# A two-layer streaming encoder: x turned by VectorE and carried through DRAM at five of six norms, blocks in another order, turned blocks issued from GpSimd

## The chip, the cores and the metric

One NeuronCore of a Trainium2 chip runs the kernel. Times are device microseconds (us). The engines are TensorE (PE: matmuls and transposes against an identity), VectorE (DVE), ScalarE (ACT), GpSimd (POOL) and SyncE (SP), which issues transfers. Each engine works its own instructions in a fixed order and waits on semaphores.

## The reference

x is (256, 1024) f32, two layers. Each layer does

```
x = x + 1/2 * SwiGLU_1(RMSNorm(x))      # D_FF = 2816
h = RMSNorm(x); [q_s|k_s|v_s|q_m] = h @ W_in
self attention (layer 0: chunked, relative bias; layer 1: differential, rotary)
memory attention: 4 heads into RMSNorm(mem) @ W_mem_kv
x = x + concat(self_out, mem_out) @ W_out
x = x + 1/2 * SwiGLU_2(RMSNorm(x))
```

with `swiglu(h) = (silu(h @ w_gate) * (h @ w_up)) @ w_down` and `rmsnorm(x, g) = x * rsqrt(mean(x^2) + eps) * g`. So six norms stand between products: three per layer.

## The kernel before

The 256 tokens are two blocks (tb 0, 1) of 128. Every dense product (`dense`) is three f32r matmuls of 128x512: each operand is split into a rounded part (h, hi) and a rest (l, lo), and hi·xh, lo·xh and hi·xl are summed in PSUM. Weights come in chunks of 1 MB (`raw`, three buffers; transfers from SyncE). A chunk has four quarters of 128x512; ACT rounds each into `hi` (L302), DVE makes `lo` (L314). There are four buffers for hi and lo, so at most four chunks are split ahead of use.

Norm and turn: a block is summed from PSUM in two halves of 512 columns (`finish`, L466 and L469). `prep_half` then turns a half by four TensorE transposes into the PSUM tile `xtp` (L396), multiplies by the gain (`y`, L427), rounds to `xh` on ACT (L430) and subtracts to `xl` on DVE (L432). The factor rsqrt(mean) is not applied to x but behind the next product: ACT squares (L441), DVE adds (`sst`, L450; `v`, L401), GpSimd takes the power (`xr`, L403).

A feed-forward runs eleven groups of 256 gate and 256 up columns (`gu`, two chunks each), eight k-steps for each block; in the first group all of block 0 goes before block 1 (but not in the first feed-forward). `evac` makes silu·up (`h`, L494), turns it by DVE in 32x32 blocks (`hb`, L503), stores it to DRAM (`hd`, L508) and loads it back with the blocks exchanged (`hr`, four loads, L514), both issued from SyncE; ACT and DVE split it to `ht`. The down product (`acc`) takes chunks 0 to 7 for all four (block, half) sums and the last three chunks (`SPLIT = NG - 3`) half by half, so that the sums of the four halves end one after the other and each norm half starts under the next. The mixer projects five column blocks (`proj`), each block 0 then block 1, runs the attention units beside them, and ends with the output product in the same manner.

The order of all instructions is written when the program is built: `Flow` keeps a clock with a cost for each operation, threads (`yield` of a time or a condition) are resumed when their condition holds on that clock, and `dense` steps it. At run time only each engine's order and the semaphores count.

Of the kernel before, what the change touches and what calls it, by code (L numbers as in the profile page):

```python
# [12 lines left out]
F32 = mybir.dt.float32  # L13
# [7 lines left out]
P = 128  # L21
# [6 lines left out]
KT = D // P  # L28
# [114 lines left out]
def kernel(  # L143
# [45 lines left out]
    load_x(0, 0)  # L189

# [61 lines left out]
    dma_free = [2.3]  # L252
# [10 lines left out]
    def loader():  # L263
        for i, c in enumerate(chunks):
# [4 lines left out]
            for j, (dst, src) in enumerate(c.parts):  # L269
                nc.sync.dma_start(out=dst(c.raw), in_=src)  # L270
                dma_free[0] += 2.9 / len(c.parts)
                if j == 1 and i < 2:
                    c.early = dma_free[0] + LAT
                    if i:
                        load_x(1, 1)
                        dma_free[0] += 0.7
            c.arrive = dma_free[0] + LAT
            if i == 0:
                load_x(1, 0)
                load_x(0, 1)  # L280
                dma_free[0] += 1.4
# [135 lines left out]
    def prep_half(xt, tb, hf, gc, wait=0.0):  # L417
        yield banks.has()
        tp = bank("xtp")
        for k in range(4):  # L420
            t = turn(tp[:, k, :], xs[tb][:, hf * 512 + k * P:hf * 512 + (k + 1) * P])
        yield t
        yield g2.has()
        y = g2.take([P, 4, P], F32, "y")
        ks = slice(hf * 4, hf * 4 + 4)
        g = gcol[:, gc + hf * 4:gc + hf * 4 + 4]
        nc.vector.tensor_tensor(out=y, in0=tp, in1=g.unsqueeze(2).broadcast_to([P, 4, P]), op=ALU.mult)  # L427
        banks.give()
# [31 lines left out]
    def finish(acc, tb, xt, gc, half):  # L460
        for hf in range(2):
            sl = slice(hf * 512, (hf + 1) * 512)
            yield lambda: acc.t[tb][hf] is not None
            yield acc.t[tb][hf]
            if half:
# [6 lines left out]
            if xt is None:  # L472
                nc.sync.dma_start(out=out[0, tb * P:(tb + 1) * P, sl], in_=xs[tb][:, sl])
            else:
                yield from prep_half(xt, tb, hf, gc)


    def ffn(l, nm, xt, gc_next):
# [3 lines left out]
        def evac(g, ps, end):  # L482
# [23 lines left out]
            hd = dram.tile([4, 32, 4, P], F32, tag="hd", name="hd")  # L506
            yield t
            nc.sync.dma_start(out=hd.rearrange("a i b x -> (a i) (b x)"), in_=hb.rearrange("p b f t j -> p (b f t j)"))  # L508
            yield flow.now + 3.0
            g2.give()  # L510
            yield g2.has()
            hr = g2.take([P, 4, 2, 2, 32], F32, "hr")
            for b in range(4):
                nc.sync.dma_start(out=hr[32 * b:32 * b + 32].rearrange("p a f t j -> p a (f t j)"),  # L514
                                  in_=hd[:, :, b, :].rearrange("a i x -> i a x"))
            yield flow.now + 4.0
            yield g4.has()
            ht = g4.take([P, 2, 4, P], F32R, "ht")
            src = hr.rearrange("p a f t j -> p (f t) a j")
# [8 lines left out]
        for g, ids in enumerate(plan[l, nm, "gu"]):  # L528
# [6 lines left out]
            for tb, c in order:  # L535
# [4 lines left out]
                if c == 1:  # L540
                    end[tb] = t
# [799 lines left out]
```

## Time and profile before

| | |
|---|---|
| median of 3 runs | 974.63 us (974.41 to 975.08) |
| profiled execution | 975.12 us, its span 973.3 us, granted clock 1.000 |
| PE, DVE, ACT, POOL busy | 99%, 69%, 56%, 6% |
| DMA | 200.90 MB, mean 206 GB/s; 65.5% of the 16 engines' span in the one queue of transfers |
| transfers of turned blocks | 44 stores of 256 KB, 176 loads of 64 KB, all from SP |
| transposes of x on PE | 96 |

A row of the timeline is: start us, us, engine line operation out<-in shape xcount, and in brackets the idle time before it with what ended it. A row of the groups by line has busy us and mean ns, then the idle time in front. A row of the windows gives for a stretch the busy time and the count of PE, PEld (weight load), DVE, ACT and POOL, the granted clock, the DMA share and GB/s.

### The profile page before, as it was taken

To read this page: it belongs to the slowest core of one execution; us is meant where nothing else is said; L and a number is where in the kernel's file an instruction comes from. 1 tells how busy PE (TensorE), PEld (TensorE's weight loads), DVE (VectorE), ACT (ScalarE), POOL (GpSimd) and SP (SyncE) were. 2 spreads that over 40 slices of the span, in tenths; PEclk is the share of its full clock that TensorE was granted. 3 is DMA by queue.
4 is the path that set the end of the run, shared out by engine and by line. 5 is a ranking of instruction groups with operands and counts; after the bars stand their busy time and mean duration, and the time that the engine had idled before them with its cause. 6 is when DMAs were issued, how large, how long until landed. Compare 5 with 4: busy or idle time off the path is not lost.

```text
span 973.3 us, 13393 instructions
## 1 busy us (share of the span) xinstructions
PE 964.6 (99%) x4576; PEld 791.3 (81%) x4576; DVE 675.7 (69%) x1485; ACT 542.4 (56%) x1159; POOL 60.1 (6%) x65
## 2 busy tenths in 40 slices
PE   9999999999999999999999999999999999999998
PEld 7888888887777888888888888888787788888886
DVE  6776675887777866666476676644989886676641
ACT  6554544766685655445445555443677764555540
POOL 0000000022210000000000000000344100000000
PEclk9999999999999999999999999999999999999999
DMA  9989766475525567887648887764641369788641
GB/s 289 306 242 270 257 225 206 162 260 173 174 87 173 163 209 223 242 263 242 235 124 252 250 252 237 253 207 136 207 140 50 125 199 284 235 251 254 226 130 44
DMA packets 164447, 200.90 MB, mean 206 GB/s; under 512 B 9433, under 2 KB 140058, under 8 KB 164378
## 3 DMA queue, kind: packets, MB, share of 16 engines
q1 hardware_dynamic: 164378, 200.04, 65.5%
q8 instruction: 36, 0.59, 0.3%
q14 instruction: 33, 0.27, 0.1%
HBM read 187.42 MB, written 12.58 MB: 205 GB/s over the span
## 4 chain that ended last, share of the span: by engine, by line
PE 91%; DVE 5%; ACT 1%; DMA 1%; issue 0%; SPq 0%; ACTq 0%
PE gu L383 16%; PE gu L386 16%; PE gu L389 16%; PE acc L386 9%; PE acc L389 9%; PE acc L383 9%; PE pj L389 3%; PE pj L383 3%; PE pj L386 3%; DVE lo L314 2%; PE xtp L396 1%; PE S L983 1%; PE AV L1064 1%; PE kv L389 1%; PE kv L386 1%; PE kv L383 1%
## 5 line engine op out<-in xcount | busy, mean ns | idle before, releaser
L314 DVE TENSOR_TENSOR lo<-raw,hi 128x512 fp32r<-128x512 f32 x656 | 416.5, 684 | 161.5 <-ACT hi L302 161.3
L302 ACT CAST hi<-raw 128x512 fp32r<-128x512 f32 x656 | 365.4, 618 | 241.3 <-PE gu L389 117.9
L389 PE MATMUL gu<-hi,xl 128*128 128x512 f32 x704 | 274.3, 390 | 0.0
L383 PE MATMUL gu<-hi,xh 128*128 128x512 f32 x704 | 274.1, 389 | 0.0
L386 PE MATMUL gu<-lo,xh 128*128 128x512 f32 x704 | 274.0, 389 | 0.0
L389 PEld LDWEIGHTS gu<-hi,xl 128*128 128x128 f32 x704 | 132.2, 188 | 27.5
L383 PEld LDWEIGHTS gu<-hi,xh 128*128 128x128 f32 x704 | 132.2, 188 | 27.3
L386 PEld LDWEIGHTS gu<-lo,xh 128*128 128x128 f32 x704 | 132.2, 188 | 27.2
L383 PE MATMUL acc<-hi,ht 128*128 128x512 f32 x352 | 137.7, 391 | 0.0
L386 PE MATMUL acc<-lo,ht 128*128 128x512 f32 x352 | 137.3, 390 | 0.2 <-DVE lo L314 0.2
L389 PE MATMUL acc<-hi,ht 128*128 128x512 f32 x352 | 137.4, 390 | 0.0
L386 PEld LDWEIGHTS acc<-lo,ht 128*128 128x128 f32 x352 | 66.1, 188 | 14.1 <-DVE lo L314 0.7
L389 PEld LDWEIGHTS acc<-hi,ht 128*128 128x128 f32 x352 | 66.1, 188 | 13.7
L383 PEld LDWEIGHTS acc<-hi,ht 128*128 128x128 f32 x352 | 66.1, 188 | 13.5
L523 DVE TENSOR_TENSOR ht<-hr,ht 128x512 fp32r<-128x512 f32 x44 | 30.3, 688 | 55.0 <-ACT ht L521 55.0
L521 ACT CAST ht<-hr 128x512 fp32r<-128x512 f32 x44 | 27.1, 617 | 69.5 <-DMA hr<-hd 69.5
L389 PE MATMUL pj<-hi,xl 128*128 128x512 f32 x160 | 64.6, 404 | 0.0
L386 PE MATMUL pj<-lo,xh 128*128 128x512 f32 x160 | 63.6, 398 | 0.0
L383 PE MATMUL pj<-hi,xh 128*128 128x512 f32 x160 | 63.6, 398 | 0.0
L491 ACT ACTIVATE sil<-gu,xr 128x256 f32<-128x256 f32 x88 | 41.4, 470 | 17.5 <-PE gu L389 17.5
L503 DVE STREAM_TRANSPOSE hb<-h 128x128 f32<-128x128 f32 x176 | 44.1, 289 | 1.2
L494 DVE SCALAR_TENSOR_TENSOR h<-gu,xr,sil 128x256 f32<-128x256 f32 x88 | 42.2, 480 | 1.6
(167 smaller groups left out, 806.5 us busy)
## 6 DMA issues: line engine op xcount, KB each, us to landing
raw<-in_ffn_w_down_dram SPq DMA_DIRECT2D x44, 1024.0 KB
raw<-in_ffn_w_gate_dram SPq DMA_DIRECT2D x86, 512.0 KB
raw<-in_ffn_w_up_dram SPq DMA_DIRECT2D x86, 512.0 KB
raw<-in_w_in_dram SPq DMA_DIRECT2D x32, 512.0 KB
hd<-hb SPq DMA_DIRECT2D x44, 256.0 KB
hr<-hd SPq DMA_DIRECT2D x176, 64.0 KB
raw<-in_w_out_dram SPq DMA_DIRECT2D x8, 1024.0 KB
raw<-in_w_mem_kv_dram SPq DMA_DIRECT2D x4, 1024.0 KB
```

What stands on the lines that cost most here:

```text
L302: nc.scalar.copy(out=c.hi[:, sl], in_=c.raw[:, sl])
L314: nc.vector.tensor_sub(c.lo[:, sl], c.raw[:, sl], c.hi.bitcast(F32)[:, sl])
L383: nc.tensor.matmul(out=ps, lhsT=xh, rhs=wh, start=start, stop=False)
L386: nc.tensor.matmul(out=ps, lhsT=xh, rhs=wl, start=False, stop=False)
L389: nc.tensor.matmul(out=ps, lhsT=xl, rhs=wh, start=False, stop=stop)
L396: nc.tensor.transpose(out=dst, in_=src, identity=flip if flipped else ident)
L491: nc.scalar.activation(sil, ps[tb][:, 0:256], AF.Silu, scale=xt.r[tb])
L494: nc.vector.scalar_tensor_tensor(out=h, in0=ps[tb][:, 256:512], scalar=xt.r[tb], in1=sil, op0=ALU.mult, op1=ALU.mult)
L503: nc.vector.transpose(out=hb[:, :, f, tb, :], in_=h[:, f * P:(f + 1) * P])
L521: nc.scalar.copy(out=hi, in_=src)
L523: nc.vector.tensor_sub(lo, src, hi.bitcast(F32))
L983: nc.tensor.matmul(out=ss[e][:, pr, :nk], lhsT=q[rows, pr, :], rhs=k[rows, pr, :], start=i == 0, stop=i == len(passes) - 1)
```

## The change

1. `through_dram` is a new function: one store and four loads, issued from GpSimd. `evac` uses it for all 44 groups. `prep_half(far=True)` turns x by four DVE transposes (`xb`), carries it through DRAM (`xr`), and multiplies by the gain from SBUF. That way is taken for both blocks at the norms behind a feed-forward (three: both mixer norms, and layer 1's first), and for block 1 alone at the two norms behind a mixer. In all GpSimd issues 300 transfers. The very first norm is as before.
2. The first two gate/up groups go block by block: block 0 of both groups, then block 1 of both (before: only the first group did). The first feed-forward keeps to k-steps with the blocks in turn. Layer 1's first two projections likewise.
3. `SPLIT = NG - 4`: the last four chunks of the down product go half by half (before: three).
4. At the start x's first half of block 1 is loaded ahead of the weights, with other start times of the four first halves; the warming matmuls are spread (not shown). At the end the output is added and stored in quarters of 256 columns, from SyncE and ACT in turn.

```diff
     load_x(0, 0)
+    load_x(1, 0)
...
-                    if i:
-                        load_x(1, 1)
-                        dma_free[0] += 0.7
             c.arrive = dma_free[0] + LAT
             if i == 0:
-                load_x(1, 0)
                 load_x(0, 1)
+                load_x(1, 1)
                 dma_free[0] += 1.4
             if i > 4 and late_done[0] < len(late_loads):
                 dst, src = late_loads[late_done[0]]
...
-    def prep_half(xt, tb, hf, gc, wait=0.0):
-        yield banks.has()
-        tp = bank("xtp")
-        for k in range(4):
-            t = turn(tp[:, k, :], xs[tb][:, hf * 512 + k * P:hf * 512 + (k + 1) * P])
-        yield t
+    def through_dram(src, name):
+
+        d = dram.tile([4, 32, 4, P], F32, tag="hd", name="hd")
+        nc.gpsimd.dma_start(out=d.rearrange("a i b x -> (a i) (b x)"), in_=src)
+        yield flow.now + 3.2
+        g2.give()
         yield g2.has()
-        y = g2.take([P, 4, P], F32, "y")
+        r = g2.take([P, 4, P], F32, name)
+        for b in range(4):
+            nc.gpsimd.dma_start(out=r[32 * b:32 * b + 32], in_=d[:, :, b, :].rearrange("a i x -> i a x"))
+        yield flow.now + 4.0
+        return r
+
+    def prep_half(xt, tb, hf, gc, wait=0.0, far=False):
         ks = slice(hf * 4, hf * 4 + 4)
         g = gcol[:, gc + hf * 4:gc + hf * 4 + 4]
-        nc.vector.tensor_tensor(out=y, in0=tp, in1=g.unsqueeze(2).broadcast_to([P, 4, P]), op=ALU.mult)
-        banks.give()
+        if far:
+            yield g2.has(2)
+            xb = g2.take([P, 4, 4, 32], F32, "xb")
+            for k in range(4):
+                nc.vector.transpose(out=xb[:, :, k, :], in_=xs[tb][:, hf * 512 + k * P:hf * 512 + (k + 1) * P])
+                t = flow.dve(128, 0.05)
+            yield t
+            xr = yield from through_dram(xb.rearrange("p b k j -> p (b k j)"), "xr")
+            yield g2.has()
+            y = g2.take([P, 4, P], F32, "y")
+            nc.vector.tensor_tensor(out=y.rearrange("p k (a j) -> p k a j", a=4),
+                                    in0=xr.rearrange("p a (k j) -> p k a j", k=4),
+                                    in1=g.unsqueeze(2).unsqueeze(3).broadcast_to([P, 4, 4, 32]), op=ALU.mult)
+            g2.give()
+        else:
+            yield banks.has()
+            tp = bank("xtp")
+            for k in range(4):
+                t = turn(tp[:, k, :], xs[tb][:, hf * 512 + k * P:hf * 512 + (k + 1) * P])
+            yield t
+            yield g2.has()
+            y = g2.take([P, 4, P], F32, "y")
+            nc.vector.tensor_tensor(out=y, in0=tp, in1=g.unsqueeze(2).broadcast_to([P, 4, P]), op=ALU.mult)
+            banks.give()
         yield flow.dve(512)
         nc.scalar.copy(out=xt.h[tb][:, ks, :], in_=y)
         yield flow.act(512)
...
-    def finish(acc, tb, xt, gc, half):
+    def finish(acc, tb, xt, gc, half, far):
         for hf in range(2):
             sl = slice(hf * 512, (hf + 1) * 512)
             yield lambda: acc.t[tb][hf] is not None
             yield acc.t[tb][hf]
+            if xt is None:
+                for q in range(2):
+                    qs = slice(hf * 512 + q * 256, hf * 512 + q * 256 + 256)
+                    nc.vector.scalar_tensor_tensor(out=xs[tb][:, qs], in0=acc.ps[tb][hf][:, q * 256:q * 256 + 256],
+                                                   scalar=0.5, in1=xs[tb][:, qs], op0=ALU.mult, op1=ALU.add)
+                    yield flow.dve(256)
+                    (nc.scalar if q else nc.sync).dma_start(out=out[0, tb * P:(tb + 1) * P, qs], in_=xs[tb][:, qs])
+                banks.give()
+                continue
             if half:
                 nc.vector.scalar_tensor_tensor(out=xs[tb][:, sl], in0=acc.ps[tb][hf], scalar=0.5, in1=xs[tb][:, sl],
                                                op0=ALU.mult, op1=ALU.add)
...
-            if xt is None:
-                nc.sync.dma_start(out=out[0, tb * P:(tb + 1) * P, sl], in_=xs[tb][:, sl])
+            if far and hf == 0:
+                flow.spawn(prep_half(xt, tb, hf, gc, far=True))
             else:
-                yield from prep_half(xt, tb, hf, gc)
+                yield from prep_half(xt, tb, hf, gc, far=far)
 
...
-            hd = dram.tile([4, 32, 4, P], F32, tag="hd", name="hd")
-            yield t
-            nc.sync.dma_start(out=hd.rearrange("a i b x -> (a i) (b x)"), in_=hb.rearrange("p b f t j -> p (b f t j)"))
-            yield flow.now + 3.0
-            g2.give()
-            yield g2.has()
-            hr = g2.take([P, 4, 2, 2, 32], F32, "hr")
-            for b in range(4):
-                nc.sync.dma_start(out=hr[32 * b:32 * b + 32].rearrange("p a f t j -> p a (f t j)"),
-                                  in_=hd[:, :, b, :].rearrange("a i x -> i a x"))
-            yield flow.now + 4.0
+            yield t
+            hr = yield from through_dram(hb.rearrange("p b f t j -> p (b f t j)"), "hr")
             yield g4.has()
             ht = g4.take([P, 2, 4, P], F32R, "ht")
-            src = hr.rearrange("p a f t j -> p (f t) a j")
+            src = hr.rearrange("p a (c j) -> p c a j", c=4)
...
-        for g, ids in enumerate(plan[l, nm, "gu"]):
+        def open_group(g):
             flow.until(banks.has(2))
-            ps = [bank(f"gu{tb}", (P, 512)) for tb in range(2)]
-            end = [None, None]
+            ps, end = [bank(f"gu{tb}", (P, 512)) for tb in range(2)], [None, None]
             flow.spawn(evac(g, ps, end))
-            order = [(tb, c) for tb in range(2) for c in range(2)] if g == 0 and (l, nm) != (0, 1) else \
-                    [(tb, c) for c in range(2) for tb in range(2)]
-            for tb, c in order:
-                for k in range(4):
-                    kk = 4 * c + k
-                    t = dense(ps[tb], xt.h[tb][:, kk, :], xt.l[tb][:, kk, :], lambda: xt.t[tb][kk], ids[c], k,
-                              lambda w: k4(w)[:, k, :], kk == 0, kk == KT - 1)
-                if c == 1:
-                    end[tb] = t
+            return g, ps, end
+
+        def run(grp, tb, kk):
+            g, ps, end = grp
+            c, k = kk // 4, kk % 4
+            t = dense(ps[tb], xt.h[tb][:, kk, :], xt.l[tb][:, kk, :], lambda: xt.t[tb][kk], plan[l, nm, "gu"][g][c], k,
+                      lambda w: k4(w)[:, k, :], kk == 0, kk == KT - 1)
+            if kk == KT - 1:
+                end[tb] = t
+
+        rest = 0
+        if (l, nm) == (0, 1):
+            grp = open_group(0)
+            for kk in range(KT):
+                for tb in range(2):
+                    run(grp, tb, kk)
+            rest = 1
+        else:
+            grps = []
+            for tb in range(2):
+                for g in range(2):
+                    if tb == 0:
+                        grps.append(open_group(g))
+                    for kk in range(KT):
+                        run(grps[g], tb, kk)
+            rest = 2
+        for g in range(rest, NG):
+            grp = open_group(g)
+            for c in range(2):
+                for tb in range(2):
+                    for k in range(4):
+                        run(grp, tb, 4 * c + k)
...
-        SPLIT = NG - 3
+        SPLIT = NG - 4
...
-            flow.spawn(finish(acc, tb, nxt, gc_next, True))
+            flow.spawn(finish(acc, tb, nxt, gc_next, True, True))
...
-        def proj(i, evac):
-            flow.until(banks.has(2))
-            ps = [bank(f"pj{tb}", (P, 512)) for tb in range(2)]
+        def proj(*parts):
+            pss = []
             for tb in range(2):
-                for c in range(2):
-                    for k in range(4):
-                        kk = 4 * c + k
+                for n, (i, evac) in enumerate(parts):
+                    if tb == 0:
+                        flow.until(banks.has(2))
+                        pss.append([bank(f"pj{j}", (P, 512)) for j in range(2)])
+                    ps = pss[n]
+                    for kk in range(KT):
+                        k = kk % 4
                         t = dense(ps[tb], xt.h[tb][:, kk, :], xt.l[tb][:, kk, :], lambda: xt.t[tb][kk],
-                                  plan[l, "in"][i][c], k, lambda w: k4(w)[:, k, :], kk == 0, kk == KT - 1)
-                flow.spawn(evac(ps[tb], tb, t))
+                                  plan[l, "in"][i][kk // 4], k, lambda w: k4(w)[:, k, :], kk == 0, kk == KT - 1)
+                    flow.spawn(evac(ps[tb], tb, t))
 
         class Heads:
             def __init__(self):
...
             flow.spawn(unit(c, tb))
-        proj(0, qk_evac(0))
-        flow.until(g4.has(2))
-        take_v()
-        proj(1, v_evac)
-        proj(2, qk_evac(1))
-        proj(3, qk_evac(2))
-        proj(4, vq_evac)
+        if typ_a:
+            proj((0, qk_evac(0)))
+            flow.until(g4.has(2))
+            take_v()
+            proj((1, v_evac))
+        else:
+            flow.until(g4.has(3))
+            take_v()
+            proj((0, qk_evac(0)), (1, v_evac))
+        proj((2, qk_evac(1)))
+        proj((3, qk_evac(2)))
+        proj((4, vq_evac))
...
-            flow.spawn(finish(acc, tb, nxt, gc_next, False))
+            flow.spawn(finish(acc, tb, nxt, gc_next, False, tb == 1))
...
-            flow.spawn(start(tb, hf, (3.75, 8.2, 7.4, 10.4)[2 * tb + hf]))
+            flow.spawn(start(tb, hf, (3.75, 9.2, 4.6, 9.9)[2 * tb + hf]))
```

What it does to the order, at two places. VectorE at layer 1's norm behind the second feed-forward of layer 0, from block 0's last `y` to the first `h` of the next product (raw, hi and lo 86 to 88 are weight chunks; acc11 the last sum; xl0, xl1 the rests of block 0 and 1). Before:

```order
L427 TENSOR_TENSOR y_4910<-xtp_4898,gcol_103 128x512
L314 TENSOR_TENSOR lo86_4905<-raw86_4746,hi86_4904 128x512 x3
L432 TENSOR_TENSOR xl1_4486<-y_4910,xh1_4484 128x512
L466 SCALAR_TENSOR_TENSOR x1_86<-acc11_4482,x1_86 128x512
L314 TENSOR_TENSOR lo86_4905<-raw86_4746,hi86_4904 128x512
L314 TENSOR_TENSOR lo87_4925<-raw87_4783,hi87_4924 128x512 x2
L427 TENSOR_TENSOR y_4962<-xtp_4949,gcol_103 128x512
L314 TENSOR_TENSOR lo87_4925<-raw87_4783,hi87_4924 128x512 x2
L314 TENSOR_TENSOR lo88_4960<-raw88_4820,hi88_4959 128x512 x2
L432 TENSOR_TENSOR xl1_4486<-y_4962,xh1_4484 128x512
L314 TENSOR_TENSOR lo88_4960<-raw88_4820,hi88_4959 128x512
L494 SCALAR_TENSOR_TENSOR h_5001<-gu0_4932,xr_4489,sil_4993 128x256
```

Now, behind the last sum's add and one quarter of lo86:

```order
L435 STREAM_TRANSPOSE xb_4996<-x1_86 128x4x32 x4
L458 TENSOR_TENSOR xl0_4531<-y_4970,xh0_4529 128x512
L312 TENSOR_TENSOR lo86_4956<-raw86_4792,hi86_4955 128x512 x3
L476 TENSOR_TENSOR sst_5023<-xss_4533 128x1
L399 TENSOR_SCALAR v_5025<-sst_5023 128x1
L441 TENSOR_TENSOR y_5033<-xr_4989,gcol_104 128x512
L312 TENSOR_TENSOR lo87_4982<-raw87_4829,hi87_4981 128x512 x4
L458 TENSOR_TENSOR xl1_4532<-y_5033,xh1_4530 128x512
L529 SCALAR_TENSOR_TENSOR h_5070<-gu0_4975,xr_4535,sil_5054 128x256
L312 TENSOR_TENSOR lo88_5021<-raw88_4966,hi88_5020 128x512
L538 STREAM_TRANSPOSE hb_5072<-h_5070 128x4x32 x2
L441 TENSOR_TENSOR y_5081<-xr_5047,gcol_104 128x512
```

The last half's `y` moved from ahead of lo87's third quarter to behind lo88's first, since its data come back through DRAM, and block 0's second `xl` now stands behind the last sum.

GpSimd's queue at the same norm holds nothing but one power per block before. Now:

```order
L418 DMA hd_4862<-xb_4851 128x512
L424 DMA xr_4880<-hd_4862 32x4x128 x4
L418 DMA hd_4899<-xb_4888 128x512
L424 DMA xr_4920<-hd_4899 32x4x128 x4
L418 DMA hd_4950<-xb_4929 128x512
L424 DMA xr_4989<-hd_4950 32x4x128 x4
L418 DMA hd_5009<-xb_4996 128x512
L401 TENSOR_TENSOR xr_4535<-v_5025,nhalf_94 128x1
L424 DMA xr_5047<-hd_5009 32x4x128 x4
L401 TENSOR_TENSOR xr_4536<-v_5103,nhalf_94 128x1
L418 DMA hd_5195<-hb_5072 128x512
L424 DMA hr_5234<-hd_5195 32x4x128 x4
```

Each half's store stands behind the loads of the half before it, and the first power of the norm between the last half's store and its loads.

More of the change, by code (lines that the diff above doesn't have):

```diff
@@ L251 @@
     hl_left = [NHL]
-    dma_free = [2.3]
+    dma_free = [4.0]
     LAT = 1.5
@@ L1259, in start_gain @@
         warm(2)
-        yield 5.0
-        warm(6)
+        for t in (5.0, 5.6, 6.2, 6.8, 7.4):
+            yield t
+            warm(2)
     def start(tb, hf, t):
```

## The prediction, made before the changed kernel ran

> **What bounds the kernel now.** I read the page first (busy time, chain of waits), then windows and TensorE's own row, then groups by line, and last the places where the edits fall.
>
> ```profile
> PE 964.6 (99%) x4576; PEld 791.3 (81%) x4576; DVE 675.7 (69%) x1485; ACT 542.4 (56%) x1159; POOL 60.1 (6%) x65
> PE 91%; DVE 5%; ACT 1%; DMA 1%; issue 0%; SPq 0%; ACTq 0%
> 440.00:480.00 40.00, 40.00 (x178) 33.11 (x178) 22.60 (x41) 18.48 (x36) 0.00 (x0) 1.00 0.75 244
> 500.00:510.00 10.00, 10.00 (x48) 8.25 (x47) 9.96 (x20) 8.33 (x18) 0.00 (x0) 1.00 0.50 151
> 690.00:780.00 90.00, 87.82 (x502) 69.29 (x502) 81.25 (x184) 64.69 (x182) 30.89 (x27) 1.00 0.40 130
> ```
>
> TensorE (PE) is 91% of the chain and never idle between 440 and 480: 178 matmuls in 40.00 us, of which one or two straddle an edge, so 0.227 each. Yet the row 500 to 510, a norm, shows VectorE (DVE) at 9.96 of 10: PE does not wait there, but DVE has nothing left to give. Only layer 1's mixer (690 to 780) shows idle PE time, 2.2 us. So an edit pays by what leaves PE's row, and costs what it puts on DVE at a norm.
>
> **What is removed: 7.04 us of PE.**
>
> ```profile
> 503.37 0.39 PE L389 MATMUL gu<-hi,xl 128*128 128x512 f32 x1
> 503.60 0.39 PE L383 MATMUL gu<-hi,xh 128*128 128x512 f32 x1
> 503.83 0.39 PE L386 MATMUL gu<-lo,xh 128*128 128x512 f32 x1
> 504.06 0.60 PE L396 MATMUL xtp<-ident,x 128*128 128x128 f32 x4
> 504.41 0.47 PE L389 MATMUL gu<-hi,xl 128*128 128x512 f32 x1
> 504.72 0.39 PE L383 MATMUL gu<-hi,xh 128*128 128x512 f32 x1
> L396 PE MATMUL xtp<-ident,x 128*128 128x128 f32 x96 | 15.0, 280 | 0.9 <-DMA x<-in_x_dram 0.9
> ```
>
> From the matmul before four turns (503.83) to the second after them (504.72) is 0.89 instead of two pitches, 0.45: a set of four costs 0.44. 96 turns are 24 sets; TensorE's order keeps 8, so 16 × 0.44 = 7.04 goes. Regrouped matmuls (the later split of the down projection, blocks, `proj`) keep their number: 0.
>
> **What is added on DVE.** Per half block four transposes of x, where y already existed.
>
> ```profile
> 502.68 0.69 DVE L466 SCALAR_TENSOR_TENSOR x<-acc,x 128x512 f32<-128x512 f32 x1
> 503.28 1.89 DVE L314 TENSOR_TENSOR lo<-raw,hi 128x512 fp32r<-128x512 f32 x3
> 505.08 0.69 DVE L427 TENSOR_TENSOR y<-xtp,gcol 128x512 f32<-128x512 f32 x1
> 505.69 2.49 DVE L314 TENSOR_TENSOR lo<-raw,hi 128x512 fp32r<-128x512 f32 x4
> 509.69 0.15 DVE L450 TENSOR_TENSOR sst<-xss 128x1 f32<-128x1 f32 x1
> 509.95 0.68 DVE L314 TENSOR_TENSOR lo<-raw,hi 128x512 fp32r<-128x512 f32 x1
> 510.55 0.50 DVE L503 STREAM_TRANSPOSE hb<-h 128x128 f32<-128x128 f32 x2
> ```
>
> Back to back a 128x512 operation starts every 0.60 (502.68, 503.28; three in 1.80), a transpose takes 0.25, so four take 1.0. Sixteen halves add 16 us of DVE, of no price in itself; what counts is when DVE's row, in its fixed order, delivers the lo quarters that PE wants next. I walk it at layer 1's first norm behind a feed-forward. Time 0 is the end of the last down matmul; the half before it ended 24 × 0.227 = 5.44 earlier (24 matmuls by the new split). DVE after that earlier end: add done −4.7, xl −4.1, transposes −3.1, four lo85 −0.7, y −0.1; then, with the last half: add 0.75, lo86's first 1.35, transposes 2.35, xl 2.95, three lo86 4.75, the two small ones 5.05, y 5.65, four lo87 8.05 (the first at 6.25), xl 8.65, h 9.05, lo88's first 9.65, two transposes 10.15, y 10.75, lo88's second 11.35.
>
> PE needs lo87's first quarter one matmul into the second group, 5.44 + 0.23 = 5.67: 0.58 late. Half a group on (2.72), lo88's first is due at 8.97, comes 9.65: 0.68. Its second is due three matmuls later, 10.33, comes 11.35: 1.02. Sum **+2.28**. Before, PE took two chunks in these 10.87 us, now four, because block 0 runs both groups; that is the price of the block order. At the mixer's norm of layer 1 the same walk, with the head sums (0.6) in place of h, gives 0.58 + 1.05 + 0.44 = **+2.07**. At layer 0's mixer norm the memory products (two stretches of 10.87) stand between: 0. At the two norms behind a mixer only block 1 goes through DRAM: layer 0 nothing, layer 1 the block-0 half's xl about 3.63 against 3.17 due, so **+0.5** (bounds 0 and 2). Transposes and y inside layer 1's mixer: 0 taken, since PE waits there anyway and DVE has 8.75 of 90 free; bounds 0 and 2.4 (four 0.6 operations).
>
> **What is moved: five transfers per group and per half to GpSimd.** The trace of before has no transfer from GpSimd, so its issue price e is bounded by what stands nearest.
>
> ```profile
> L514 SPq DMA_DIRECT2D hr<-hd x176: 312/427/1487, 30.8 to 916.5; - x176
> L403 POOL TENSOR_TENSOR mr<-v,nhalf 128x1 f32<-128x1 f32 x2 | 1.1, 550 | 163.1 <-DVE v L401 163.1
> L403 POOL TENSOR_TENSOR xr<-v,nhalf 128x1 f32<-128x1 f32 x12 | 8.8, 732 | 435.6 <-DVE v L401 435.6
> L403 POOL TENSOR_TENSOR of<-v,nhalf 128x2 f32<-128x2 f32 x6 | 5.9, 991 | 21.9 <-DVE v L401 21.9
> 510.18 0.86 POOL L403 TENSOR_TENSOR xr<-v,nhalf 128x1 f32<-128x1 f32 x1 [10.67 <-DVE v L401]
> 419.28 0.34 SPq L508 DMA_DIRECT2D hd<-hb  x1
> 421.32 1.75 SPq L514 DMA_DIRECT2D hr<-hd  x4
> 427.09 0.62 ACT L521 CAST ht<-hr 128x512 fp32r<-128x512 f32 x1 [4.08 <-DMA hr<-hd]
> 343.17 1.75 SPq L514 DMA_DIRECT2D hr<-hd  x4
> 346.64 0.62 ACT L521 CAST ht<-hr 128x512 fp32r<-128x512 f32 x1 [1.85 <-DMA hr<-hd]
> ```
>
> Low bound 0.43 (SyncE's issue), high 0.99 (a two-column GpSimd operation). I take 0.73, GpSimd's smallest operation in the very norms concerned. The store lands 421.32 − 419.28 − 0.34 = 1.70 after its issue; the loads 346.64 − 344.92 = 1.72 after their last issue, or 4.02 where weights stand ahead on SyncE's queue. On a queue of its own the first is nearer; with some share for the weights I take 2.2. A transport then takes 5e + 1.70 + 2.2 = 7.55, and holds GpSimd's queue 5e + 1.70 = 5.35, under the 5.44 between halves. The last half's store is issued at 2.45, lands at 10.0; DVE comes to its y at 10.15. It fits, barely: 0, as long as e stays under 0.75. GpSimd's own work queued behind (the two rsqrt per norm, the next group's five transfers) then moves by under one transport and the down projection uses those much later. The evacuation's transfers in the other groups are equally far from their use: 0, because the down projection starts only when all groups are through.
>
> By the Trainium skill (DMA: Bandwidth & Descriptors, "Queues, rings and completion order") each transfer engine turns between queues packet by packet, which would favour 1.72 over 4.02; no run here shows it yet. With 4.02 instead the sum would be 1.67 worse at each of four norms, as worked in the first rival.
>
> **Start and end.** x's first half of block 1 now stands ahead of the weights and warming matmuls are spread; 256 KB at the 289 GB/s of the page's first slice are 0.9, so 0 with bounds ±0.9. At the end the last add covers half the columns and is followed by its own store:
>
> ```profile
> 969.57 0.69 DVE L466 SCALAR_TENSOR_TENSOR x<-acc,x 128x512 f32<-128x512 f32 x1 [3.39 <-PE acc L389]
> 970.28 0.33 SPq L473 DMA_DIRECT2D out_dram<-x  x1
> GB/s 289 306 242 270 257 225 206 162 260 173 174 87 173 163 209 223 242 263 242 235 124 252 250 252 237 253 207 136 207 140 50 125 199 284 235 251 254 226 130 44
> ```
>
> Half of 0.69 can be won, another issue (0.33) lost: 0.
>
> **Sum.** −7.04 + 2.28 + 2.07 + 0.5 = −2.2. The profiled execution took 975.12 (span 973.3), so 972.9; the median of the three runs, 974.63, gives **972.4**.
>
> **Rivals.**
>
> *The transport comes late (slower).* Place: y of the last half in DVE's order, behind which lo88 waits, and behind that PE. For it: the row at 510.18, where the same rsqrt takes 0.86 rather than 0.55 beside a lo on DVE (509.95), and DVE is full at every norm. Against it: the mean there is 0.73. Past e = 0.75 a queue of four halves loses 5e + 1.70 − 5.44 at each of three intervals. At 0.86: 3 × 0.56 + (2.45 + 8.20 − 10.15) = 2.2 at each of two norms, 1.05 at each norm behind a mixer (one interval): +6.5 − 2.2 = +4.3, so 978.9. At 0.99: 4.8 and 2.35, +14.3 − 2.2, so **986.7**. It decides the sign from e = 0.79. Loads that land in 4.02 with e = 0.73 cost 1.67 four times: 979.1.
>
> By the Trainium skill (SBUF — State Buffer, "SBUF: two separate sides") a VectorE operation with two operands in SBUF shuts out a GpSimd instruction that reads SBUF, and certain VectorE operations starve transfers that GpSimd issues. The 0.86 agrees with the first half; no row here bears on the second. By it the result is this rival's 978.9 or more.
>
> *DVE loses nothing (full gain).* If operations ready early let lo run ahead of my walk, the stalls vanish: −7.04, so **967.6**. For: no PE wait at 500 to 510 although DVE is at 9.96. Against: twice the chunks in the same time. That the turns don't leave at all is ruled out by TensorE's order.
>
> **How the numbers follow.** Forecast 0.52, late transport 0.30, full gain 0.18. Within 0.2% (1.95 us, about what can be told from no change) the forecast lies just outside, so I split it 0.28 faster, 0.17 same, 0.07 slower; the late transport is 0.28 slower and 0.02 same. Faster 0.46, same 0.19, slower 0.35. The forecast's own range comes from its unknowns (start ±0.9, layer 1's entry −0.5 to +1.5, its mixer up to +2.4, seldom all at once): about 970.5 to 976. The range reaches from 966 (full gain and a good start) to 987 (e = 0.99).
>
> **What would show it.** Eight sets of turns in PE's groups; PE waits for lo of about 0.6, 0.7 and 1.0 in the second group behind the two norms of layer 1; GpSimd's issue in its queue's row (0.73; past 0.79 I am wrong in sign); y's release by DVE itself, not by a transfer; no PE wait at layer 0's mixer. Wrong I am if waits stand ahead of the down projection, or if DVE's transposes of x take longer than 0.25.

## The result: 8% slower

The changed kernel takes 1054.03 us in the median of 6 runs (1046.55 to 1057.57), the kernel before 974.77 in 6 runs beside it: a ratio of 1.0804, 95% interval 1.0769 to 1.0838. Forecast were 972.4 and a range up to 987. The profiled execution is the fastest of the six, with a span of 1044.8 us, so that its parts below add up to 71 us of loss and not to the 79 of the medians.

The page of the changed kernel, its busy times, its chain of waits, and three of its groups by line; the last row is the same group in the kernel before:

```profile
PE 984.9 (94%) x4520; PEld 791.3 (76%) x4520; DVE 682.6 (65%) x1553; ACT 534.2 (51%) x1159; POOL 225.0 (22%) x365
PE 32%; DMA 27%; ACT 12%; issue 11%; DVE 11%; POOL 6%; ACTq 0%; DVEq 0%; POOLq 0%
DMA hr<-hd 16%; ACT hi L300 9%; POOL hr L424 5%; DVE lo L312 5%; PE gu L381 4%; PE gu L387 4%; PE gu L384 4%; PE acc L384 3%; PE acc L387 3%; DMA hd<-hb 3%; PE acc L381 3%; DMA xr<-hd 2%; DMA hd<-xb 2%; PE pj L381 2%; PE pj L384 2%
...
L547 ACT CAST ht<-hr 128x512 fp32r<-128x512 f32 x44 | 27.3, 620 | 279.3 <-DMA hr<-hd 279.3
L441 DVE TENSOR_TENSOR y<-xr,gcol 128x512 f32<-128x512 f32 x16 | 11.0, 688 | 35.7 <-DMA xr<-hd 35.7
L394 PE MATMUL xtp<-ident,x 128*128 128x128 f32 x32 | 5.5, 309 | 0.0
```

```profile
L521 ACT CAST ht<-hr 128x512 fp32r<-128x512 f32 x44 | 27.1, 617 | 69.5 <-DMA hr<-hd 69.5
```

TensorE was 91% of the chain and is 32%. The longest other piece is not a norm: it is `hr<-hd`, the loads of the groups' turned blocks. ACT stood idle for 279.3 us ahead of the 44 casts that take them up, 6.3 each; before it was 69.5, 1.6 each. VectorE's wait for the halves of x is 35.7 over all 16. The turns did leave: 32 are left of 96.

Where the time went is read from TensorE's rows, part by part: from the first dense matmul of a part to the first of the next, in us of the profiled executions. The experiments below stand beside it.

| part | before | the change | e4: groups planned by landing | e1: all from SyncE | e7: e1 without the halves' way | e12: e1, 3 chunks held, weights held back | e16: one norm only |
|---|---|---|---|---|---|---|---|
| start | 9.0 | 8.9 | 8.3 | 8.4 | 8.6 | 8.4 | 8.7 |
| layer 0: gate/up 1 | 121.3 | 128.9 | 121.9 | 125.8 | 126.0 | 126.1 | 121.5 |
| down 1 | 63.7 | 79.2 | 68.0 | 67.6 | 69.1 | 62.2 | 63.7 |
| memory products | 23.0 | 28.9 | 28.8 | 29.7 | 25.6 | 33.1 | 23.0 |
| projections, attention | 71.4 | 71.4 | 71.4 | 71.4 | 71.4 | 71.6 | 71.4 |
| output product | 32.4 | 31.9 | 31.9 | 31.9 | 32.4 | 31.9 | 31.9 |
| gate/up 2 | 120.2 | 122.7 | 124.1 | 124.7 | 120.2 | 119.7 | 119.7 |
| down 2 | 61.3 | 66.6 | 59.8 | 59.8 | 61.3 | 60.1 | 61.3 |
| layer 1: gate/up 1 | 120.2 | 129.3 | 124.0 | 125.0 | 120.2 | 121.7 | 120.2 |
| down 1 | 61.3 | 66.1 | 59.8 | 59.8 | 61.3 | 60.6 | 61.3 |
| projections, attention | 73.3 | 77.9 | 78.5 | 75.9 | 68.0 | 69.4 | 73.3 |
| output product | 32.4 | 33.3 | 33.3 | 33.3 | 37.0 | 38.0 | 31.6 |
| gate/up 2 | 120.2 | 129.6 | 125.9 | 126.2 | 120.2 | 121.7 | 120.2 |
| down 2, to the end | 63.8 | 70.1 | 63.8 | 63.7 | 63.7 | 63.7 | 63.8 |

Every feed-forward is longer, its down product too, and that far from any norm. One group of layer 0 in the timeline of the changed kernel (POOL is GpSimd, SPq SyncE's queue):

```profile
104.01 0.56 POOL L418 DMA_DIRECT2D hd<-hb  x1 [10.23 <-DVE hb L538]
104.92 0.37 SPq L271 DMA_DIRECT2D raw<-in_ffn_w_gate_dram  x1
105.33 0.57 SPq L271 DMA_DIRECT2D raw<-in_ffn_w_up_dram  x1
106.70 2.17 POOL L424 DMA_DIRECT2D hr<-hd  x4 [2.13 <-DMA hd<-hb]
107.33 0.37 SPq L271 DMA_DIRECT2D raw<-in_ffn_w_gate_dram  x1
107.74 0.51 SPq L271 DMA_DIRECT2D raw<-in_ffn_w_up_dram  x1
116.47 0.62 ACT L547 CAST ht<-hr 128x512 fp32r<-128x512 f32 x1 [8.99 <-DMA hr<-hd]
117.00 3.22 ACT L300 CAST hi<-raw 128x512 fp32r<-128x512 f32 x6
118.72 0.56 POOL L418 DMA_DIRECT2D hd<-hb  x1 [9.85 <-DVE hb L538]
```

and the same group in the kernel before:

```profile
101.63 0.34 SPq L508 DMA_DIRECT2D hd<-hb  x1
103.78 1.80 SPq L514 DMA_DIRECT2D hr<-hd  x4
110.81 0.62 ACT L521 CAST ht<-hr 128x512 fp32r<-128x512 f32 x1 [0.56 <-DMA hr<-hd]
112.60 0.34 SPq L508 DMA_DIRECT2D hd<-hb  x1
```

From the store's issue to ACT's cast it was 9.18, with ACT waiting 0.56 of it. Now it is 12.46, and ACT waits 8.99. The issue price is a small part of it: the five issues took 2.14 and take 2.73. The loads are issued while two chunks of weights, 2 MB, are in flight or follow, and on another queue than those. In the trace's packet records the first packet of these loads comes 3.5 us after their issue, when the chunk ahead of them has gone, and then their 256 KB share the transfer engines with the next chunk for 5.3 us. Behind the cast, ACT has the weight casts (117.00, six at once) that TensorE and the raw buffers wait for. The next group's store follows 14.7 later, before 10.97 (101.63 to 112.60).

This closes a circle: a store, its late loads, ACT's cast, the weight casts and VectorE's work behind it, the next store. Over the 44 groups the cast came 8.9 us behind its store in the median before, and comes 11.4 behind it now; ACT was through with what stands ahead of the cast 8.3 us behind the store before, and 3.5 now. In the group shown TensorE loses nothing yet (14.00 of 14.00 us busy between 104 and 118), since it lives on chunks that were split ahead. It pays later, 0.69 behind the next cast, and more in the down product, behind the one after that:

```profile
146.60 0.62 ACT L547 CAST ht<-hr 128x512 fp32r<-128x512 f32 x1 [9.67 <-DMA hr<-hd]
147.13 3.22 ACT L300 CAST hi<-raw 128x512 fp32r<-128x512 f32 x6
147.79 0.50 PE L381 MATMUL acc<-hi,ht 128*128 128x512 f32 x1 [1.65 <-ACT hi L300]
```

Over the first feed-forward gate/up and down product together lose 23 us by the table. Not all of it is the groups': with their casts written later (e4 below) 4.9 of the 23 stay.

### The profile page after: what moved, and what is told of

It reads as the page before. It is cut to its first block, busy times and chain, and to the rows that moved or that the text cites. A ratio compares the mean times of both kernels' runs of the same rounds, so it can differ in the third digit from the quotient of the medians.

```text
span 1044.8 us, 13542 instructions
## 1 busy us (share of the span) xinstructions
PE 984.9 (94%) x4520; PEld 791.3 (76%) x4520; DVE 682.6 (65%) x1553; ACT 534.2 (51%) x1159; POOL 225.0 (22%) x365
## 4 chain that ended last, share of the span: by engine, by line
PE 32%; DMA 27%; ACT 12%; issue 11%; DVE 11%; POOL 6%; ACTq 0%; DVEq 0%; POOLq 0%
DMA hr<-hd 16%; ACT hi L300 9%; POOL hr L424 5%; DVE lo L312 5%; PE gu L381 4%; PE gu L387 4%; PE gu L384 4%; PE acc L384 3%; PE acc L387 3%; DMA hd<-hb 3%; PE acc L381 3%; DMA xr<-hd 2%; DMA hd<-xb 2%; PE pj L381 2%; PE pj L384 2%
## 5 line engine op out<-in xcount | busy, mean ns | idle before, releaser
L312 DVE TENSOR_TENSOR lo<-raw,hi 128x512 fp32r<-128x512 f32 x656 | 412.7, 681 | 32.4 <-ACT hi L300 32.2
L381 PE MATMUL gu<-hi,xh 128*128 128x512 f32 x704 | 277.0, 393 | 9.1 <-ACT xh L456 6.1
L547 ACT CAST ht<-hr 128x512 fp32r<-128x512 f32 x44 | 27.3, 620 | 279.3 <-DMA hr<-hd 279.3
L381 PE MATMUL acc<-hi,ht 128*128 128x512 f32 x352 | 140.5, 399 | 12.9 <-ACT hi L300 12.8
L384 PE MATMUL acc<-lo,ht 128*128 128x512 f32 x352 | 141.9, 403 | 9.2 <-DVE lo L312 8.3
L387 PE MATMUL acc<-hi,ht 128*128 128x512 f32 x352 | 139.1, 395 | 0.0
L424 POOL DMA_DIRECT2D hr<-hd x176 | 95.7, 550 | 127.2 <-ACT hi L300 56.5
L381 PEld LDWEIGHTS acc<-hi,ht 128*128 128x128 f32 x352 | 67.3, 191 | 31.5 <-ACT hi L300 17.6
L418 POOL DMA_DIRECT2D hd<-hb x44 | 25.0, 567 | 307.0 <-DVE hb L538 306.8
L387 PEld LDWEIGHTS acc<-hi,ht 128*128 128x128 f32 x352 | 67.4, 191 | 13.0
L456 ACT CAST xh<-y 128x512 fp32r<-128x512 f32 x24 | 14.7, 618 | 79.0 <-DVE y L441 68.4
```

The lines of the kernel that those rows point to most:

```text
L312: nc.vector.tensor_sub(c.lo[:, sl], c.raw[:, sl], c.hi.bitcast(F32)[:, sl])
L381: nc.tensor.matmul(out=ps, lhsT=xh, rhs=wh, start=start, stop=False)
L384: nc.tensor.matmul(out=ps, lhsT=xh, rhs=wl, start=False, stop=False)
L387: nc.tensor.matmul(out=ps, lhsT=xl, rhs=wh, start=False, stop=stop)
L418: nc.gpsimd.dma_start(out=d.rearrange("a i b x -> (a i) (b x)"), in_=src)
L424: nc.gpsimd.dma_start(out=r[32 * b:32 * b + 32], in_=d[:, :, b, :].rearrange("a i x -> i a x"))
```

## Experiments

Theory G: the groups' transfers cost, on a queue of their own beside the weights, through ACT's order. Theory N: the norms' new way costs.

**e1: all transfers from SyncE.**

```diff
 def through_dram(src, name):
-        nc.gpsimd.dma_start(out=d...., in_=src)
+        nc.sync.dma_start(out=d...., in_=src)
...
-            nc.gpsimd.dma_start(out=r[32 * b:32 * b + 32], ...)
+            nc.sync.dma_start(out=r[32 * b:32 * b + 32], ...)
```

> The change with all 300 transfers of turned blocks issued from SyncE instead of GpSimd, nothing else. Theory G (the groups' transfers are what costs: on a queue of their own they share the transfer engines with the weights, land late, and ACT's cast of ht holds the weight casts behind it): the 79 us go, 966 to 978. Theory N (the norms' new way through DRAM, with its extra VectorE work, is what costs): stays above 1030.

Measured: 1005.01, ratio 1.0298 (1.0281 to 1.0315). 49 us are gone, 30 stay: neither expectation held, each theory has a part.

**e2: groups from SyncE, norms from GpSimd.**

```diff
+        eng = nc.sync if name == "hr" else nc.gpsimd     # hr: a group's block
```

> The change with the 220 transfers of the 44 groups issued from SyncE, the 80 of the norms still from GpSimd. Theory G: 970 to 990. Theory N: above 1030.

Measured: 1001.71, ratio 1.0278 (1.0255 to 1.0301). That is above G's range and far under N's. The some 50 us belong to the groups; for the norms the queue makes hardly a difference.

**e3: the kernel before, groups from GpSimd.**

```diff
-            nc.sync.dma_start(out=hd....)
+            nc.gpsimd.dma_start(out=hd....)
...
-                nc.sync.dma_start(out=hr[32 * b:...])
+                nc.gpsimd.dma_start(out=hr[32 * b:...])
```

> The kernel before with only the 220 transfers of the 44 groups issued from GpSimd. Theory G: 1040 to 1065, alone as slow as the whole change. Theory N: 970 to 980.

Measured: 1041.82, ratio 1.0682 (1.0666 to 1.0698). Five transfers per group on another queue, and nothing else, cost 67 us, in G's range.

**e4: the change with one planner number altered.**

```diff
-        yield flow.now + 4.0
+        yield flow.now + (9.5 if name == "hr" else 4.0)
```

> The change with one planner number altered: the groups' loads are taken to need 9.5 instead of 4.0, so that ACT's cast of ht is written behind more weight casts; every transfer is still issued from GpSimd and lands as late. Theory G says that the late landing costs only through ACT's order: 970 to 1000. If the late landing costs by itself, or by less bandwidth for the weights: above 1030.

Measured: 1002.95, ratio 1.0284 (1.0268 to 1.03), 3 us past G's range and as good as moving the groups back. ACT's group in this kernel:

```profile
L547 ACT CAST ht<-hr 128x512 fp32r<-128x512 f32 x44 | 27.2, 617 | 0.0
```

ACT waits 0.0 us for the 44 loads though all still come from GpSimd, and three of the four down parts in the table are as in the kernel before or shorter (59.8, 59.8, 63.8); the first stays at 68.0, as with the groups on SyncE (67.6 in e1). The late landing cost only by the place where ACT's order took it up: that is what the groups cost. The rest, 28 us, is elsewhere.

**e10 and e11: the kernel before, only loads or only stores from GpSimd.**

```diff
-                nc.sync.dma_start(out=hr[32 * b:...])      # e10
+                nc.gpsimd.dma_start(out=hr[32 * b:...])
...
-            nc.sync.dma_start(out=hd....)                  # e11
+            nc.gpsimd.dma_start(out=hd....)
```

> The kernel before with the 176 loads hr issued from GpSimd, the 44 stores still from SyncE. Theory: the loads are the part that drains slowly beside the weights (5 us with about 1 MB of weights running, 2.2 us with none), so they carry nearly all of the 67 us: 1025 to 1045. Rival (GpSimd's issue and start of any transfer): half, about 1000 to 1015.

> The kernel before with the 44 stores hd issued from GpSimd, the loads still from SyncE. Theory: 974 to 985. Rival: about 1000 to 1015.

Measured: loads 1018.0, ratio 1.0421 (1.0375 to 1.0467); stores 975.54, ratio 1.0001 (0.999 to 1.0013). Stores from GpSimd are free, loads cost 43 of the 67, between the two ranges expected for them. Both together cost 24 more than the sum. The traces show a likely reason, not tested apart: in the median the cast comes 11.0 us behind the store's issue in e10 and 11.5 in e3, so once ACT waits for the loads, the store's part of the way counts too; with the loads on SyncE (e11) it is 8.6, and 8.9 before.

**The second part: e5 to e8.** Theory W: the four held down chunks and the block order stop the weights ahead of a norm. Theory F: the halves' way through DRAM is late by itself.

```diff
-        SPLIT = NG - 4          # e5: e1 with three chunks held
+        SPLIT = NG - 3
...
-            for tb in range(2):  # e6: e1, block order in the first group only,
-                for g in range(2):  # and one projection after the other
+            for tb in range(2):
...
-            flow.spawn(finish(acc, tb, nxt, gc_next, True, True))    # e7: e1, turns on TensorE
+            flow.spawn(finish(acc, tb, nxt, gc_next, True, False))
```

e8 is the kernel before with `through_dram` (from SyncE), `prep_half(far=True)` and the `far` of `finish` as the change has them, and nothing else of it.

> The all-SyncE version of the change with three instead of four down chunks kept for the half-by-half end, as before. Theory W (four held chunks fill all four hi and lo buffers, so no weight is split or fetched for 17 us ahead of a norm, and weights and turned halves then come together): gains most of the rest, 975 to 988. Theory F (the halves' way through DRAM is late by itself, since VectorE's y stands in its order ahead of lo): 1000 or more, because the halves now follow each other in 4.08 instead of 5.44.

> The all-SyncE version with only the first group block by block, as before, and the projections as before; four chunks still held. Theory W: a part of the rest, 985 to 998, since two chunks fewer are wanted in the first 10.87 us. Theory F: 995 to 1005.

> The all-SyncE version with all turns of x on TensorE again (the transposes come back: 7.0 us); blocks in the new order, four held chunks, new start and end stay. Theory F: the norms' loss goes, 975 to 985. Theory W: the loss stays, 995 to 1012.

> The kernel before with only the halves of the five norms turned by VectorE and carried through DRAM, all from SyncE; split, order of groups, start and end as before. Theory F: 985 to 1005. Theory W: 966 to 978.

Measured: e5 991.15, ratio 1.0161 (1.0141 to 1.0182); e6 1012.06, 1.0379 (1.0356 to 1.0402); e7 985.27, 1.0103 (1.0086 to 1.012); e8 1015.23, 1.0405 (1.0378 to 1.0431). All four miss the ranges: e5 lies between the two, e6 above both, e7 0.3 us and e8 10 us beyond F's. Still F holds for the larger part: without the halves' way (e7) the gate/up parts behind a norm are exactly as before, 120.2, block order and all; with nothing but it (e8) 40 us are lost. The block order does not cost: without it (e6) the halves' lateness costs 7 more. W has a part too, 14 us in e5. Where a half is late, all edits interact. Layer 1's first norm in e1, from the timelines of VectorE, SyncE and TensorE, and three windows:

```profile
516.26 0.34 SPq L418 DMA_DIRECT2D hd<-xb  x1
518.72 0.40 SPq L271 DMA_DIRECT2D raw<-in_ffn_w_gate_dram  x1
519.16 0.51 SPq L271 DMA_DIRECT2D raw<-in_ffn_w_up_dram  x1
519.71 3.04 SPq L424 DMA_DIRECT2D xr<-hd  x4
524.86 0.40 PE L381 MATMUL gu<-hi,xh 128*128 128x512 f32 x1
527.08 0.69 DVE L441 TENSOR_TENSOR y<-xr,gcol 128x512 f32<-128x512 f32 x1 [2.77 <-DMA xr<-hd]
527.69 2.49 DVE L312 TENSOR_TENSOR lo<-raw,hi 128x512 fp32r<-128x512 f32 x4
528.43 0.80 PE L384 MATMUL gu<-lo,xh 128*128 128x512 f32 x1 [3.17 <-DVE lo L312]
529.02 0.63 PE L387 MATMUL gu<-hi,xl 128*128 128x512 f32 x1
529.45 0.63 PE L381 MATMUL gu<-hi,xh 128*128 128x512 f32 x1
```

```profile
526.00:529.00 3.00, 0.57 (x1) 0.50 (x2) 1.92 (x4) 2.83 (x6) 0.00 (x0) 0.90 1.02 347
529.00:532.00 3.00, 3.00 (x9) 2.35 (x8) 3.00 (x7) 0.85 (x3) 0.00 (x0) 0.54 0.51 98
532.00:535.00 3.00, 3.00 (x14) 2.24 (x13) 2.96 (x6) 1.25 (x3) 0.00 (x0) 1.00 0.96 328
```

The half's store is issued at 516.26, its loads stand behind 1 MB of weights on SyncE and land at 527.08, 10.8 after the store. VectorE has stood there, and lo behind it, and TensorE behind lo. The same length shows in the change itself from GpSimd:

```profile
531.86 0.56 POOL L418 DMA_DIRECT2D hd<-xb  x1
536.73 0.56 POOL L418 DMA_DIRECT2D hd<-xb  x1
538.73 0.68 DVE L441 TENSOR_TENSOR y<-xr,gcol 128x512 f32<-128x512 f32 x1
547.57 0.69 DVE L441 TENSOR_TENSOR y<-xr,gcol 128x512 f32<-128x512 f32 x1 [3.52 <-DMA xr<-hd]
548.92 0.50 PE L384 MATMUL gu<-lo,xh 128*128 128x512 f32 x1 [3.95 <-DVE lo L312]
```

The second half, stored at 531.86 with no weights in flight, is taken up at 538.73, after 6.9; the third, stored at 536.73 with weights, at 547.57, after 10.8.

**e9: block order and quarters at the end alone.** Without any new transfer, three chunks held, start as before.

```diff
-    finish(..., far=True), SPLIT = NG - 4, new start
+    finish(..., far=False), SPLIT = NG - 3, start of before
```

> The change without its transfers: turns on TensorE, groups from SyncE, three held chunks, start as before; left of it are the block order of the first two groups and of layer 1's projections, and the end in quarters. If block order costs nothing (theory: the 2.28 and 2.07 that the prediction charged to it do not exist) 972 to 976. If they exist: 977 to 981.

Measured: 978.58, ratio 1.0034 (1.0021 to 1.0048), in the band that was to confirm the block order's price, and yet not by it: the gate/up parts behind norms are 120.2, 120.2 and 120.3 as before. Nearly the whole excess stands in the first gate/up (124.4 against 121.3), where TensorE waits 1.43 for x, having waited for it ahead of this part already, and 1.43 at the turn of the gain columns, one transpose of small loaded vectors. This turn stands behind 296 gate/up matmuls in TensorE's order, before and here alike; what moved is the last small load that it needs, which stands among the weights on SyncE and is issued at 72.3 before, at 75.6 here and at 77.3 in the changed kernel:

```profile
81.96 0.24 PE L231 MATMUL gps<-ident,grow 55*128 55x55 f32 x1 [4.62 <-DMA grow<-in_b_subln_dram]
```

In e3, with TensorE's order and the start of before, the load is issued at 80.7 and the wait is 7.70; in e4 there is none. So the groups' lateness alone can make it.

**e12: weights held back between a half's store and its loads.** e5 with

```diff
-            yield lambda: raw_left[0] > 0
+            yield lambda: raw_left[0] > 0 and hold[0] == 0     # hold: set from store to loads of a half
```

> The all-SyncE version with three held chunks, and in SyncE's order no weight transfer between a half's store and its loads at the five norms. Theory (a half turned through DRAM is late because its loads stand behind 1 MB of weights on SyncE's queue): 975 to 986, against 991 without the hold. If the loads are late by themselves, or the weights then are: 988 to 1000.

Measured: 990.12, ratio 1.0146 (1.0124 to 1.0167), in the rival's range. Yet the gate/up behind layer 0's mixer falls from 125.3 to 119.7, under the kernel before; the sum hides it behind other places: the gain columns, and the memory products at 33.1, where TensorE waits 7.9 for the normed memory keys (`kmn`), VectorE's work.

**e13 and e14: planner numbers by the measured landing.**

```diff
-        yield flow.now + 4.0                     # loads of a half, e13 on e12; e14 on e4 with three chunks held
+        yield flow.now + 7.5
...
-        yield flow.now + 8.0                     # gain columns
+        yield flow.now + 20.0
```

> As the version with weights held back (990), and two planner numbers nearer to the measured landing: a half's loads are taken to need 7.5 instead of 4.0, so that VectorE's y is written behind more of its other work, and the turn of the gain columns is written 12 us later. Theory (what is left of the loss is VectorE and TensorE standing at a transfer that the plan took to be there, above all 10 us at layer 0's mixer norm and 3 to 5 us at the gain columns): 974 to 982. Rival (TensorE itself needs the halves before they can land): 986 to 992.

> The change with all transfers from GpSimd as it stands, but planned by measured landings (groups' loads 9.5, halves' loads 7.5, gain columns 12 us later) and three held chunks. Theory (order, not the transfers, makes the loss): 976 to 990. Rival (shared transfer engines cost by themselves): 995 or more.

Measured: 1001.08, ratio 1.0262 (1.0242 to 1.0282), and 1016.55, ratio 1.043 (1.041 to 1.045): both worse than the kernels they start from, and e14 in its rival's range: the theory of order alone fell for the norms. Written later, the halves are taken later, and TensorE waits for xh itself (4.23 in one stretch ahead of layer 1's first gate/up in both), and for the memory keys 9.3 in e13 and 12.6 in e14. Only the gain columns were mended: the first gate/up is 121.1 and 121.4.

**e15: four held chunks, with all that was mended.** e12 with `SPLIT = NG - 4`, the gain columns' turn later, the memory's preparation at its old place.

> The all-SyncE change with its own split (four held chunks), no weight transfer between a half's store and its loads at the norms, the memory's preparation at its old place behind down chunk 6 and the gain columns' turn 12 us later. Theory (four held chunks give the halves their time, 5.44 apart, but stop the weights; three let the weights go on and leave the halves late): both costs stay apart from the mended ones, 984 to 992. If the hold alone was missing: 966 to 976.

Measured: 991.3, ratio 1.0157 (1.0142 to 1.0171), at the upper end of what was expected: no split serves both. With four chunks held the first gate/up of layer 1 loses (126.9) to late lo, and the down product ahead of the memory's norm stays long (67.4); with three (e12) that is 62.2, but layer 0's memory products lose more (33.1 against 30.6).

**e16: the one norm that gained.** The edit against the change, in short:

```diff
-        finish(acc, tb, nxt, gc_next, True, True) ... finish(acc, tb, nxt, gc_next, False, tb == 1)
+        finish(acc, tb, nxt, gc_next, True, False) ... finish(acc, tb, nxt, gc_next, False, tb == 1 and l == 0)
...
+        hold as in e12; SPLIT = NG - 3; gain columns + 20.0; layer 1's projections as before; all from SyncE
```

> Block order of the first two groups, new start and end, gain columns' turn 12 us later, three held chunks, groups from SyncE; of the five norms only block 1 behind layer 0's mixer is turned by VectorE through DRAM, from SyncE with the weights held back. That is the one place where the phase times show a gain (0.9 us of turns). If it stays: 973.3 to 974.8, a little under the kernel before. If the other edits still cost: 975 to 979.

Measured, 11 runs: 973.43, ratio 0.9978 (0.9969 to 0.9987): a little faster than the kernel before and the best of all. By the table 0.9 of it is this norm (31.9 for 32.4 and 119.7 for 120.2); layer 1's output product (31.6 for 32.4, but 31.7 in e11 too) and the start give the rest, and neither has a half that goes through DRAM. SyncE and VectorE at that norm, and then the same place in e5:

```profile
319.91 3.22 SPq L419 DMA_DIRECT2D hd<-xb  x2
323.23 3.71 SPq L426 DMA_DIRECT2D xr<-hd  x8
327.04 0.40 SPq L272 DMA_DIRECT2D raw<-in_ffn_w_gate_dram  x1
327.83 0.65 DVE L444 TENSOR_TENSOR y<-xr,gcol 128x512 f32<-128x512 f32 x1
```

```profile
329.49 3.22 SPq L418 DMA_DIRECT2D hd<-xb  x2
333.55 0.38 SPq L271 DMA_DIRECT2D raw<-in_ffn_w_gate_dram  x1
334.59 1.99 SPq L424 DMA_DIRECT2D xr<-hd  x4
343.01 0.69 DVE L441 TENSOR_TENSOR y<-xr,gcol 128x512 f32<-128x512 f32 x1 [5.49 <-DMA xr<-hd]
```

With the loads ahead of the weights VectorE takes the half at 327.83 and waits for nothing, 7.9 after the first store; with one chunk between them at 343.01, 13.5 after. Block 0's matmuls, 10.87, cover the one and not the other.

## Why the prediction was wrong, point by point

- **The failed step: "The evacuation's transfers in the other groups are equally far from their use: 0".** Their use is not the down product but ACT's cast, which has a fixed place in ACT's order ahead of weight casts. The trace of before showed that there was no cover: ACT already waited for these loads, 69.5 us over 44 casts and 0.56 in the group above, so a later landing is a later cast. The price is 49 to 52 us in the change (e1, e2), 67 alone (e3), and none to be seen once the cast is written later (e4). The prediction's own sign of being wrong came: TensorE waits for hi ahead of and in the down products. The prediction itself asks what is queued behind a waiting instruction; it asked it at the norms and not at the 44 groups.
- **The landing.** The step took 2.2 us for a half's loads, near the 1.72 of a place without weights, because the queue was its own. Without weights that is right: 6.9 from store to use, 7.55 predicted. With weights it is 10.8 on either queue. The row with 4.02, where weights stood ahead, was the nearer one: an own queue did not take the transfers past the weights. The prediction read the rule of the Trainium skill (DMA: Bandwidth & Descriptors, "Queues, rings and completion order") in favour of the early landing; the packet records do not bear that reading out. The loads' first packet comes 2.4 us after issue in the median of the 47 cases where 1 MB of weights or more runs (1.3 in the 6 where none does), and the last ends after 7.3 (3.4). It is the weights and not VectorE: the loads issued at 534.50, with VectorE busy throughout and no weights, have their first packet after 1.3.
- **The issue price e** was right in kind: 0.55 for a load, 0.56 for a store, under my 0.73 and under the point of 0.75. The first rival, a late transport, had the right mechanism at the norms. Its cause was not e; its row of 4.02 pointed the right way, at a price of 6.7. The halves' way costs 19.7 net in the SyncE version (e1 against e7), although 7 us of turns leave.
- **The norm walk, +2.28 and +2.07**, rested on transfers being there. It is not confirmed: block order without transfers adds nothing at these norms (e7, e9), and with them the loss is larger and everywhere: in e1 4.8 in layer 1's first gate/up, 3.5 in its mixer, and 4.5 and 6.0 at the two norms behind a mixer, where +0.5 was forecast for both together. What VectorE's 0.9 for four transposes would add with prompt transfers no run shows apart.
- **The turns, −7.04**: right. They leave (32 of 96 remain), and where nothing else is late the parts show it: 59.8 for 61.3, 31.9 for 32.4.
- **Layer 0's mixer norm, 0, since the memory products cover it**: wrong. They take 28.9 instead of 23.0, 29.7 in e1, and 25.6 without the halves' way (e7). VectorE stands at a half's `y` in its fixed order, the memory keys behind it are late, and TensorE waits for them:

```profile
227.32 0.69 DVE L441 TENSOR_TENSOR y<-xr,gcol 128x512 f32<-128x512 f32 x1 [3.90 <-DMA xr<-hd]
233.20 0.69 PE L394 MATMUL kmtp<-ident,kmn 128*128 128x128 f32 x2 [3.38 <-DVE kmn L640]
```

- **Start, 0 ± 0.9**: holds, the first dense matmul comes at 8.9 instead of 9.0. Behind it the sum has no term for the gain columns' turn, which waits 4.62 in the change and 2.40 in e1, where the first gate/up loses 4.5.
- **SPLIT, 0**: wrong. Four held chunks cost about 5 in the down product ahead of the memory's norm (67.6 in e1, 62.2 with three), and more behind norms: e5 against e1 is 14 us.

The sum, by medians: 49.0 for the queue, nearly all the groups' (the change against e1; 52.3 against e2), 19.7 for the halves' way after its gain of 7 (e1 against e7), 10.5 for the rest (e7 against the kernel before), which by the table lies in the first gate/up (4.7), the down product behind it (5.4) and the memory products (2.6), less what the other parts give back. Together 79.2. As the edits interact, another order of taking them out would share it otherwise.

## What to carry to other kernels

A transfer moved to another queue is costed at its consumer's place in that engine's order: if the consumer waits already (0.56 here), there is no cover, and what stands behind it is late too. The way through DRAM paid at the one norm where its loads went ahead of the weights and the next product covered some 8 us; a queue of its own did not buy that. When transfers land at other times, check every instruction with a fixed place that waits for one, such as the gain columns here.

## What was not expected of the hardware

- The groups' loads from GpSimd were issued at a steady 0.55 us, whatever VectorE did beside them; of the slowing by VectorE that the rule of the Trainium skill in the prediction (SBUF — State Buffer, "SBUF: two separate sides") allows for, the issue shows nothing. The loads of the changed kernel, with shortest, median and longest issue in ns:

```profile
L424 POOL DMA_DIRECT2D hr<-hd x176: 548/548/569, 30.9 to 1000.9; - x176
```

- A wait of TensorE was paid a second time by its clock. After the 3.17 us above, the granted clock is 0.54 between 529 and 532, nine matmuls start in 3 us, and it is 1.00 again from 532. In the change the mean clock is 0.985: at most 15.7 of the 1044.8 us, an estimate from those two numbers.
